# Three transfers of a recurrence's substitution step, issued on GpSimd's queue and no longer on SyncE's

## Chip, cores and metric

The kernel runs on one core of a Trainium2 chip. The metric is the device time of one execution in microseconds (us), given as the median of several runs; lower is better.

## What is computed

The reference runs two blocks of two layers each on 512 tokens of width 1024 in float32. The part that matters here is the first layer of the second block: a recurrence over the tokens with 12 heads of size 64, run forwards and backwards, over 256 context tokens and then 512 more.

```python
def rwkv7_scan(r, w, k, v, kk, bb, s0, reverse):
    def step(s, inp):
        r_t, w_t, k_t, v_t, kk_t, b_t = inp
        sa = jnp.einsum('bhij,bhj->bhi', s, kk_t)
        s = s * w_t[:, :, None, :] - sa[..., None] * b_t[:, :, None, :] + v_t[..., None] * k_t[:, :, None, :]
        return s, jnp.einsum('bhij,bhj->bhi', s, r_t)
```

The rest (projections, gated normalisations, a windowed attention, a pooling layer, two feed-forward layers and a retention layer) lies before and after this stage.

## The kernel before

The program is written with a layer that takes the engine of every instruction from the code, adds the waits between instructions itself and chooses, at build time, the order in which each engine meets its instructions. Every engine works through its own queue in that order. All transfers of the kernel are issued by SyncE (`nc.sync`).

The recurrence (`rwkv`, L1288) works in chunks of 64 tokens. Two heads form a pair; there are six pairs, and each pair has three groups of four chunks for each of the two directions, which makes 18 passes, numbered from 0 here. The loop at L1401 runs pass q: it weaves, one step of each in turn, the chain of states of pass q (`chain`, L1797), the second half of the inversion for pass q+1 (`inner_rest`, L1691, and `inner_second`, L1740), the products of pass q+2 (`products`, L1634, and `keys_by_token`, L1678) and the vectors of pass q+3 (`inner_first`, L1567). The recurrence inside a chunk asks for the inverse of 16 triangular systems of size 64 x 64 (two directions, two heads, four chunks). Between these, `Feed` (L2120) puts matmuls of the projections of later pairs (L363 to L365), whose weight panels are loaded at L349 into two buffers `ws`.

One inversion takes this way. TensorE makes the products (L1648), VectorE masks them into `M` (L1652). SyncE stores the 16 systems to a scratch tensor `lt` in device memory (L1659, two transfers) and loads from it the 64 diagonal blocks of 16 x 16, one on each of 64 partitions, into `sN` (L1662). GpSimd inverts these by substitution: thirty operations (L1670, L1671) on `sX`, `sO` and `sN`, which have one buffer each, after two operations that set `sX` to the unit matrix (L1665, L1666). It then writes the transposed copy `sT` (L1664, called at L1673). Both are stored to a scratch tensor `td` (L1675, `sT` first in the code). One step of the weaving later, `inner_rest` loads `td` back as 64 x 64 matrices, `T` from the transposed one and `DB` from the other, two transfers each (L1733). GpSimd also clears `VU` in that function (L1701, two operations), which has two buffers and so waits for products of an earlier `chain` (L1862). `inner_second` completes the inverse from the blocks with matmuls of L1757: the first group multiplies with `T`, the second with `DB`. `chain` uses the result.

Of the kernel before, what the change touches and what calls it, by code (L numbers as in the profile page):

```python
# [273 lines left out]
class Program:  # L274
# [1013 lines left out]
    def rwkv(self, hl, hc):  # L1288
# [3 lines left out]
        with tc.tile_pool(name="rk", bufs=1) as rp:  # L1292
# [176 lines left out]
            def leading():  # L1469

                for j, tags in enumerate((("acc0", "acc1"), ("acc0", "c"), ("u", "c"))):
                    lead.append([self.psum(t)[:, :n] for t, n in zip(tags, (T, TC))])
                    for p0, ks in ((0, (0, 1, 2, 3)), (4, (4, 6, 7))):
                        pan = self.panel(out[j], p0, 4)
                        for k in ks:
                            products(j, pan, p0, (k,))
                            yield
# [6 lines left out]
            for j in range(3):  # L1484
                products(j, self.panel(out[j], NH2 - 1, 1), NH2 - 1, (NH2 - 1,))
# [148 lines left out]
    def products(self, g, st):  # L1634

        nc, rp = self.nc, self.rp
        tt = nc.vector.tensor_tensor
        half = lambda i: slice(64 * i, 64 * i + 64)

        M = st["M"] = rp.tile([P, 2, 2, 4, P], F32, tag="m", name="m", bufs=3)  # L1640

        e2 = lambda ap: ap.rearrange("p (c e) t -> p c e t", e=2)
        for d in range(2):
            pss, last = [self.psum("c", (P, 4, P)) for _ in range(2)], None
            for j in range(4):
                i = 2 - 2 * (j % 2)
                for h in (1, 0):
                    last = self.queue(nc.tensor.matmul(  # L1648
                        pss[h][:, j, :], st["BK"][d][half(h), j, :, :].rearrange("p s t -> p (s t)"),
                        st["AR"][d][half(h), j // 2, i:i + 2, :].rearrange("p s t -> p (s t)"), start=True, stop=True), last)  # L1650
            for h in range(2):
                tt(out=e2(M[:, d, h]), in0=e2(pss[h]), in1=self.k_pmask[:, d].unsqueeze(1).to_broadcast([P, 2, 2, P]), op=ALU.mult)  # L1652
                yield

        lt, td = self.scratch[self.flip]
        self.flip = 1 - self.flip
        system = lambda e: M.rearrange("p d h (j e) t -> p e (d h) j t", e=2)[half(1 - e), e, :, :, half(e)]
        for e in range(2):
            nc.sync.dma_start(out=lt[e::2, :4096].rearrange("u (s t) -> s u t", t=64), in_=system(e))  # L1659
        N, X, XT, o = (rp.tile([64, 16, 16], F32, tag=t, name=t) for t in ("sN", "sX", "sT", "sO"))  # L1660
        blocks = lambda ap: ap.rearrange("u (b f) -> (u b) f", f=1040)[:, :1024].rearrange("q (s t) -> q s t", t=64)[:, :, :16]
        nc.sync.dma_start(out=N, in_=blocks(lt))  # L1662
        pt = nc.gpsimd.tensor_tensor
        copy = lambda out, in_: nc.gpsimd.tensor_scalar(out=out, in0=in_, scalar1=1.0, scalar2=None, op0=ALU.mult)  # L1664
        nc.gpsimd.memset(X, 0.0)  # L1665
        nc.gpsimd.memset(X.rearrange("p s t -> p (s t)")[:, ::17], 1.0)  # L1666
        for j in range(15, 0, -1):
            ob = o[:, :j, :16 - j]
            sh = [64, j, 16 - j]
            pt(out=ob, in0=N[:, :j, j:j + 1].to_broadcast(sh), in1=X[:, j:j + 1, j:].to_broadcast(sh), op=ALU.mult)  # L1670
            pt(out=X[:, :j, j:], in0=X[:, :j, j:], in1=ob, op=ALU.subtract)  # L1671

        copy(XT, X.rearrange("p s t -> p t s"))  # L1673
        for k, x in ((1, XT), (0, X)):
            nc.sync.dma_start(out=blocks(td[k]), in_=x)  # L1675
        st["td"], st["system"] = td, system

    def keys_by_token(self, st):  # L1678
# [543 lines left out]
```

## Time and profile before

| | |
|---|---|
| median of 3 runs | 2342.03 us (2341.47 to 2350.18) |
| profiled execution | 2327.58 us |
| its span, first to last instruction | 2325.8 us |
| mean granted TensorE clock | 0.971 |
| TensorE busy | 2169.9 us (93%) |
| VectorE busy | 1623.5 us (70%) |
| ScalarE busy | 1077.7 us (46%) |
| GpSimd busy | 343.7 us (15%) |
| transfers | 269.66 MB, all but 2.57 MB of instructions on SyncE's queue |

PE is TensorE's matmuls, PEld its weight loads, DVE VectorE, ACT ScalarE, POOL GpSimd and SP SyncE; a q behind an engine's name is its queue (SPq). Issuing a transfer is not counted as busy. `T<-td` reads: `T` is written, `td` is read. L12 is line 12 of the kernel. All times of the trace are counted from the start of the span.

### The profile page before, as it was taken

To read this page: it belongs to the slowest core of one execution; us is meant where nothing else is said; L and a number is where in the kernel's file an instruction comes from. 1 tells how busy PE (TensorE), PEld (TensorE's weight loads), DVE (VectorE), ACT (ScalarE), POOL (GpSimd) and SP (SyncE) were. 2 spreads that over 40 slices of the span, in tenths; PEclk is the share of its full clock that TensorE was granted. 3 is DMA by queue.
4 is the path that set the end of the run, shared out by engine and by line. 5 is a ranking of instruction groups with operands and counts; after the bars stand their busy time and mean duration, and the time that the engine had idled before them with its cause. 6 is when DMAs were issued, how large, how long until landed. Compare 5 with 4: busy or idle time off the path is not lost. (4 is left out here: it accounts for less than half of the span.)

```text
span 2325.8 us, 40219 instructions
## 1 busy us (share of the span) xinstructions
PE 2169.9 (93%) x15774; PEld 1735.8 (75%) x15774; DVE 1623.5 (70%) x3014; ACT 1077.7 (46%) x2033; POOL 343.7 (15%) x722
## 2 busy tenths in 40 slices
PE   6889989999998999999988998999999999999996
PEld 4667768878775888888666776777777777888885
DVE  6799886568859688444666868778867456555544
ACT  3466353223344332333554556546465255655542
POOL 1321020000003000000003443332424100000001
PEclk9999999999999999999999999989999999999998
DMA  8433446566623656323333232322222252422211
GB/s 288 145 128 127 135 152 197 180 220 194 193 76 115 217 187 201 109 92 90 115 100 76 44 74 47 70 46 62 56 50 54 85 177 90 131 68 73 73 55 46
DMA packets 203742, 269.66 MB, mean 116 GB/s; under 512 B 125216, under 2 KB 137376, under 8 KB 203168
## 3 DMA queue, kind: packets, MB, share of 16 engines
q1 hardware_dynamic: 203552, 267.09, 37.9%
q8 instruction: 124, 2.03, 0.4%
q14 instruction: 66, 0.54, 0.1%
HBM read 250.38 MB, written 16.66 MB: 115 GB/s over the span
## 5 line engine op out<-in xcount | busy, mean ns | idle before, releaser
L363 PE MATMUL acc<-hh,wh 128*128 128x512 f32 x1416 | 572.2, 405 | 39.6 <-ACT wh L322 24.9
L365 PE MATMUL acc<-hh,wl 128*128 128x512 f32 x1416 | 569.9, 403 | 8.0 <-POOL wl L340 4.6
L364 PE MATMUL acc<-hl,wh 128*128 128x512 f32 x1416 | 570.9, 403 | 1.8 <-DVE hl L340 1.7
L322 ACT ACTIVATE wh<-ws 128x1024 fp32r<-128x1024 f32 (+4 forms) x307 | 275.5, 901 | 412.0 <-PE acc L364 309.7
L340 DVE TENSOR_TENSOR wl<-ws,wh 128x1024 fp32r<-128x1024 f32 (+3 forms) x294 | 305.3, 1041 | 189.4 <-ACT wh L322 185.8
L363 PEld LDWEIGHTS acc<-hh,wh 128*128 128x128 f32 x1416 | 270.2, 191 | 100.1 <-ACT wh L322 28.1
L365 PEld LDWEIGHTS acc<-hh,wl 128*128 128x128 f32 x1416 | 270.0, 191 | 74.0 <-DVE wl L340 8.0
L364 PEld LDWEIGHTS acc<-hl,wh 128*128 128x128 f32 x1416 | 270.8, 191 | 60.0 <-issue 6.3
L447 DVE SCALAR_TENSOR_TENSOR ws<-ws,cact 128x1024 f32<-128x1024 f32 x144 | 180.5, 1256 | 78.1 <-DMA ws<-in_ada_dram 77.2
L363 PE MATMUL acc<-gh,wh 128*128 128x512 f32 x352 | 137.9, 392 | 2.4 <-ACT gh L322 2.4
L365 PE MATMUL acc<-gh,wl 128*128 128x512 f32 x352 | 138.1, 392 | 1.8 <-DVE wl L340 1.8
L364 PE MATMUL acc<-gl,wh 128*128 128x512 f32 x352 | 138.0, 392 | 0.3 <-DVE gl L340 0.3
L322 ACT ACTIVATE a<-a 128x512 f32<-128x512 f32 x44 | 27.8, 633 | 186.4 <-DVE a L988 186.1
L1670 POOL TENSOR_TENSOR sO<-sN,sX 64x15 f32<-64x15 f32 (+2 forms) x270 | 84.8, 314 | 182.3 <-DMA sN<-lt 162.9
L1671 POOL TENSOR_TENSOR sX<-sX,sO 64x15 f32<-64x15 f32 (+2 forms) x270 | 87.1, 322 | 21.0
L2025 POOL TENSOR_TENSOR raw<-raw,k_axial 128x512 f32<-128x512 f32 x16 | 21.9, 1366 | 413.9 <-ACT raw L322 413.9
L365 PEld LDWEIGHTS acc<-gh,wl 128*128 128x128 f32 x352 | 66.5, 189 | 16.8 <-DVE wl L340 3.1
L363 PEld LDWEIGHTS acc<-gh,wh 128*128 128x128 f32 x352 | 66.5, 189 | 16.6 <-ACT gh L322 2.8
L364 PEld LDWEIGHTS acc<-gl,wh 128*128 128x128 f32 x352 | 66.5, 189 | 14.7 <-DVE gl L340 1.0
L447 DVE SCALAR_TENSOR_TENSOR ada<-ws,cact 128x1024 f32<-128x1024 f32 x48 | 58.7, 1222 | 25.9 <-DMA ws<-in_ada_dram 25.8
L1848 DVE SCALAR_TENSOR_TENSOR S<-sp,gc,gs 64x64 f32<-64x64 f32 x240 | 58.7, 279 | 21.1 <-PE sp L1840 19.1
L363 PE MATMUL acc<-hc,wh 128*128 128x256 f32 x208 | 66.3, 319 | 4.2 <-ACT wh L322 3.8
(581 smaller groups left out, 4308.8 us busy)
## 6 DMA issues: line engine op xcount, KB each, us to landing
ws<-in_ada_dram SPq DMA_DIRECT2D x144, 512.0 KB, 4.3
ws<-in_up_dram SPq DMA_DIRECT2D x88, 512.0 KB, 4.1
ws<-in_od_in_dram SPq DMA_DIRECT2D x44, 512.0 KB, 3.5
ws<-in_ev_in_dram SPq DMA_DIRECT2D x60, 256.0 KB, 2.9
ws<-in_down_dram SPq DMA_DIRECT2D x32, 384.0 KB, 3.1
ws<-in_w_in_dram SPq DMA_DIRECT2D x22, 512.0 KB, 4.3
ws<-in_down_dram SPq DMA_DIRECT2D x32, 320.0 KB, 3.0
ws<-in_ev_in_dram SPq DMA_DIRECT2D x18, 512.0 KB, 3.5
```

What stands on the lines that cost most here:

```text
L322: ins = self.nc.scalar.activation(out=out, in_=in_, func=func, **k)
L340: (engine or self.nc.vector).tensor_tensor(out=lo, in0=x, in1=hi.bitcast(F32), op=ALU.subtract)
L363: nc.tensor.matmul(ps, wh[:, s], xh, start=start, stop=False)
L364: nc.tensor.matmul(ps, wh[:, s], xl, start=False, stop=False)
L365: nc.tensor.matmul(ps, wl[:, s], xh, start=False, stop=stop)
L447: nc.vector.scalar_tensor_tensor(out=w, in0=ws, scalar=1.0, in1=c, op0=ALU.mult, op1=ALU.mult, accum_out=d[:, m:m + 1])
L1670: pt(out=ob, in0=N[:, :j, j:j + 1].to_broadcast(sh), in1=X[:, j:j + 1, j:].to_broadcast(sh), op=ALU.mult)
L1671: pt(out=X[:, :j, j:], in0=X[:, :j, j:], in1=ob, op=ALU.subtract)
L1848: nc.vector.scalar_tensor_tensor(out=nxt[H, d, H], in0=sp[H, d], scalar=gd, in1=gs[H, d, H], op0=ALU.mult, op1=ALU.add)
L2025: nc.gpsimd.tensor_tensor(out=raw, in0=raw, in1=self.k_axial[:, 0, :], op=ALU.mult)
```

## The change

The load of the diagonal blocks (`sN` from `lt`) and the two stores of the inverted blocks (`sT` and `sX` to `td`) are issued by GpSimd. The order in the code, the buffers, the shapes and all other transfers stay as they are; the stores to `lt` (L1659) and the loads `T` and `DB` from `td` (L1733) stay on SyncE.

```diff
         N, X, XT, o = (rp.tile([64, 16, 16], F32, tag=t, name=t) for t in ("sN", "sX", "sT", "sO"))
         blocks = lambda ap: ap.rearrange("u (b f) -> (u b) f", f=1040)[:, :1024].rearrange("q (s t) -> q s t", t=64)[:, :, :16]
-        nc.sync.dma_start(out=N, in_=blocks(lt))
+        nc.gpsimd.dma_start(out=N, in_=blocks(lt))
...
         copy(XT, X.rearrange("p s t -> p t s"))
         for k, x in ((1, XT), (0, X)):
-            nc.sync.dma_start(out=blocks(td[k]), in_=x)
+            nc.gpsimd.dma_start(out=blocks(td[k]), in_=x)
```

## Rows read from the trace of the kernel before

**Rows 1.** Busy time by engine (x instructions), granted clock, DMA share, GB/s; recurrence stage

```profile
1210.00:1840.00 630.00, 587.09 (x8102) 453.54 (x8103) 480.79 (x1178) 334.61 (x773) 214.80 (x624) 0.94 0.27 61
```

**Rows 2.** Waits of engines in 1210:1840: us in total, times, longest us

```profile
PE c L1757 <- DMA T<-td: 12.9, 10, 5.3
...
ACT wh L322 <- DMA ws<-in_ev_in_dram: 2.1, 1, 2.1
```

**Rows 3.** Timeline of TensorE, L1757: start, us, in brackets the idle time before

```profile
1246.57 0.42 PE L1757 MATMUL c<-T,LB 64*64 64x32 f32 x2 [5.35 <-DMA T<-td]
...
1548.40 1.91 PE L1757 MATMUL c<-T,LB 64*64 64x32 f32 x30 [1.05 <-DMA T<-td]
1553.50 0.75 PE L1757 MATMUL c<-EC,DB 64*64 64x32 f32 x10
...
1817.75 0.27 PE L1757 MATMUL c<-T,LB 64*64 64x32 f32 x2 [1.88 <-DMA T<-td]
```

**Rows 4.** Chain of work that ended last, pass 9: start us, us, what

```profile
1521.23 0.61 DVE m L1652
...
1522.51 2.61 DMA lt<-m
...
1525.18 2.61 DMA sN<-lt
...
1540.18 1.34 POOL sT L1664
1541.54 2.50 DMA td<-sT
...
1544.69 3.67 DMA T<-td
1548.40 1.91 PE c L1757 x30
```

**Rows 5.** SyncE's waits in 1210:1840: us in total, times, longest us

```profile
SPq L1675 <- POOL sX L1671: 130.0, 16, 17.2
...
SPq L1662 <- DMA lt<-m: 23.1, 13, 2.8
...
SPq L1675 <- POOL sT L1664: 15.8, 17, 7.0
```

**Rows 6.** Issues by line: ns min/median/max; then landing of L1659, of L1662 (us)

```profile
L1659 SPq DMA_DIRECT2D lt<-m x36: 589/626/671, 1219.3 to 1792.2; - x36
...
DMA to landing us min/median/max: 2.6/2.7/3.7
...
L1662 SPq DMA_DIRECT2D sN<-lt x18: 586/592/1111, 1223.3 to 1795.1; - x18
...
DMA to landing us min/median/max: 2.6/2.9/4.3
```

**Rows 7.** Timeline of SyncE: issues of passes 3 and 4

```profile
1311.84 0.59 SPq L1662 DMA_DIRECT2D sN<-lt  x1
...
1339.08 1.28 SPq L1659 DMA_DIRECT2D lt<-m  x2
...
1344.41 0.60 SPq L1662 DMA_DIRECT2D sN<-lt  x1
```

**Rows 8.** Single operations of GpSimd and VectorE from timeline and line view (copy: ns)

```profile
1318.25 0.22 POOL L1670 TENSOR_TENSOR sO<-sN,sX 64x15 f32<-64x15 f32 x1
...
1257.30 0.30 POOL L1670 TENSOR_TENSOR sO<-sN,sX 64x64 f32<-64x64 f32 x1
1257.67 0.31 POOL L1671 TENSOR_TENSOR sX<-sX,sO 64x64 f32<-64x64 f32 x1
...
L1664 POOL TENSOR_SCALAR sT<-sX x18: 1060/1074/1335, 1240.0 to 1811.1; 64x256 f32<-64x256 f32 x18
...
1353.30 1.01 DVE L1631 SCALAR_TENSOR_TENSOR ks<-r,pcol,ks 128x768 f32<-128x768 f32 x1
1353.41 1.06 POOL L1671 TENSOR_TENSOR sX<-sX,sO 64x64 f32<-64x64 f32 x1
```

**Rows 9.** Timeline of GpSimd, first operations of passes 0, 1, 3 and 17

```profile
1226.50 0.40 POOL L1670 TENSOR_TENSOR sO<-sN,sX 64x15 f32<-64x15 f32 x1 [62.93 <-DMA sN<-lt]
...
1252.43 0.22 POOL L1670 TENSOR_TENSOR sO<-sN,sX 64x15 f32<-64x15 f32 x1 [9.38 <-DMA sN<-lt]
...
1317.18 1.09 POOL L1701 MEMSET VU<- 64x512 f32 x2 [19.16 <-PE misc L1862]
...
1798.11 0.44 POOL L1670 TENSOR_TENSOR sO<-sN,sX 64x15 f32<-64x15 f32 x1 [9.23 <-DMA sN<-lt]
```

## The prediction

> **What bounds the kernel now.** I first read the busy times by stage. The only stage that runs the changed lines is the recurrence, from 1210 to 1840 us. There TensorE is busy 587.09 of 630 us and GpSimd 214.80 [rows 1], so this stage holds 43 us of TensorE idle time, and the change can neither win more than that nor touch the rest of the program. Next I read the waits of the stage: TensorE waits 12.9 us for the transfer `T<-td`, ten times, and only 2.1 us can be laid to a weight panel that came late (ScalarE's wait on `ws`) [rows 2]. The ten waits belong to eight of the eighteen passes; the timeline has the first at 1246.57 and the last at 1817.75 [rows 3]. The other ten passes show no wait for it.
>
> Then the chain of work that ended last, which goes back no further than 1521 us. It opens with a pass of the substitution: mask product, store to `lt`, load of `sN`, thirty GpSimd operations, the copy to `sT`, store to `td`, load of `T`, and the first matmuls of L1757: 27.2 us from 1521.23 to 1548.40 with nothing beside it [rows 4]. All three moved transfers belong to this path, two of them directly: `sN<-lt` and `td<-sT`.
>
> Last, SyncE's own waits. It stands 130.0 us waiting for the last subtraction, 15.8 us for the copy to `sT` and 23.1 us for `lt` to land [rows 5]. That looks like much, but SyncE is not what the stage waits for: the late panels above come to 2.1 us.
>
> **The change, part by part.** Each pass moves three issues, 54 in all.
>
> 1. *Off SyncE.* 54 issues of 0.59 us [rows 6] are 32 us of SyncE's time, and the waits of rows 5 go with them. Part of these waits moves to the next in line: the loads `T<-td` and `DB<-td` stay on SyncE and need the stores landed. Queued behind a waiting SyncE are panel loads, the loads of saved context and `lt` stores. What these cost TensorE now is the 2.1 us above, and once `sN` is asked for late in one of the eight passes: the second store to `lt` goes out at about 1339.7, lands some 2.7 us later [rows 6], and the load follows only at 1344.41 [rows 7], 2.0 us late. The gain is 4 us.
>
> 2. *Onto GpSimd.* Each transfer has 1,024 pieces of 64 bytes (64 partitions of 16 rows of 16 numbers). No row shows GpSimd issuing one. Let g be the time one issue takes there, and x = g - 0.59 what it adds to the path. At the cheap end g is SyncE's own 0.59 us, x = 0. By GpSimd's plain operations, 0.22 us for 15 elements and 0.30 for 64 [rows 8], a step is 1.6 ns, and 1,024 steps with a start of 0.2 us make g = 1.9. By its transposing copy, 1.07 us for 256 elements [rows 8], a step is 3.4 ns after the same start, g = 3.7 and x = 3.1. If the reading and the writing side are made one after the other, g = 7.2 and x = 6.6: the dear end. Making a list of scattered addresses lies between the plain operation and the copy, so I take 2.8 us, x = 2.2 (estimates from these rows).
>
>  The queue choice has a price in the Trainium skill too (DMA: Bandwidth & Descriptors, "Latency and other measured facts"): first byte after about 1 us when GpSimd issues, against about 0.6 from SyncE's kind of queue; no run so far shows it here. By that page x would be 0.4 and the sum below about 1 us.
>
> 3. *The load of `sN`.* GpSimd now waits for `lt` itself. What stands behind that wait, the two clearings of `VU` and the thirty operations, stood behind the wait on `sN` before. In five of the eight passes GpSimd is idle until `sN` lands (the first and the last stand in [rows 9]), so x counts fully: 5x. In the other three GpSimd is held by the clearing of `VU`, which waits for TensorE: in the first of them `sN` is asked for at 1311.84, lands 2.9 us later, and the clearing ends at 1318.27 [rows 6, 7, 9], which covers x up to 3.5. I take these three at nothing; without that cover they cost 3x.
>
> 4. *The store of `sT`* comes right behind the copy on GpSimd and delays `T` by x in all eight passes: 8x.
>
> 5. *The store of `sX`* now goes second, so `DB` lands about g after `T`. The first product that reads `DB` begins at 1553.50, 5.1 us after the products with `T` start [rows 3]: covered up to g of about 5. The clearing of `sX` for the next pass waits longer for this store; in pass 1 GpSimd idles 9.38 us after that clearing [rows 9], against 2 × 2.8 us of new issues. Covered, and gone where g passes 4 or so.
>
> Sum: 13x - 4 = 13 × 2.2 - 4 = 25 us. The profiled execution took 2327.58 us, 1.8 more than its span of 2325.8, and would take 2352; it lies 14.5 below the median of the runs, 2342.03, so against that I forecast **2367 us**, 1.1% slower. At x = 0 the sum is -4 (2338), at 3.1 it is +36 (2378). At the dear end the covers of parts 3 and 5 go as well: 16 × 6.6 - 4 = 102 (2444).
>
> **Rivals.** Half a per cent, 11.7 us, is what a measurement here can tell from no change; all chances below use it.
>
> *No change* (2338 to 2353). GpSimd issues about as cheaply as SyncE, x below 1.2; 13 × 1.2 - 4 = 12. Or the build, which orders TensorE's queue by its own estimate of arrivals, puts other matmuls ahead of L1757; then the path is longer but TensorE is not idle. Against it: the 27 us of rows 4 are serial, and TensorE has only this stage's projections left to put there. The page named above supports this rival. 0.27. Should the change not do what it says (GpSimd's transfers served just as SyncE's are), it ends here too.
>
> *Faster.* SyncE free of 169 us of waits lets `lt` stores and loads go earlier, and TensorE's waits for `T` vanish with the late panel: 12.9 + 2.1 = 15, to 2327. It decides where an issue on GpSimd is cheaper than the hop to SyncE, that is with x below about -0.6. For it: the size of rows 5. Against it: in the traced pass the store starts 0.02 us after the copy ends, and the load starts 0.65 us after the store has landed, of which 0.59 is its own issue [rows 4, 6], so there is hardly a hop to save. 0.13.
>
> *Much slower* (2444). The issue on GpSimd is held up or made in two rounds. GpSimd's operations are already stretched beside VectorE: the 64-element subtraction that takes 0.31 us alone took 1.06 while VectorE ran L1631 for 1.01 [rows 8]. If each issue waited like that, 0.75 us more, x rises to 3.0 and the sum to 35. The Trainium skill (SBUF — State Buffer, "SBUF: two separate sides") says that GpSimd cannot write its transfer descriptors while VectorE holds the port that they share; the stretched row agrees for operations, and none shows it for transfers. Only with the dear end of part 2 does it become 102. 0.15.
>
> *My forecast*, slower by 12 to 75 us: 0.45.
>
> **The numbers.** Slower holds forecast and dear rival, 0.60; same 0.27; faster 0.13. The range goes from 2328, which leaves out about half of the faster rival, to 2430, which leaves out most of the dear one: about 2 in 10 outside. Its own part for the likeliest case is 2354 to 2417.
>
> **What would show it.** In the changed profile GpSimd's queue should show 54 issues, their mean being g; 0.6 kills part 2, above 4 makes the dear rival. From the end of the copy to the landing of `td<-sT`, now 2.5 us, should be 2.5 + x. TensorE's waits for `T` should grow from 12.9 by about 13x = 29, or, if the order of the build took it up, stay while the stage still grows. SyncE's waits of rows 5 should turn into waits of L1733 for `td`. I am wrong if the stage keeps its 630 us with g above 2, or if it shrinks: then SyncE's standing still did cost TensorE something that the waits lay elsewhere.

## The result, and the profile after

The changed kernel took 2376.45 us (median of 4 runs, 2372.21 to 2381.43) against 2341.75 us for the kernel before on the same chip (median of 4): the ratio is 1.0139, with a 95% interval of 1.0099 to 1.0179. It is 34.7 us slower. Ratios and intervals, here and below, come from the runs in the chip's usual state alone and are not the quotients of the medians, from which they differ by up to 0.2%. The profiled executions differ by more, 2372.21 against 2327.58 us, because the one of before lies 14 us below its median and the other only 4.

All of it is in the recurrence. From 1210 us to the first use of `T` in the last pass the kernel before takes 608 us. This is the row of before for that stretch (columns as in [rows 1]: length, busy time of TensorE, its weight loads, VectorE, ScalarE, GpSimd, then the granted clock, DMA share and GB/s), with two later slices in which the clock is at its lower level:

```profile
1210.00:1818.00 608.00, 565.09 (x7794) 436.32 (x7794) 471.35 (x1153) 329.59 (x759) 214.80 (x624) 0.95 0.26 59
...
1540.00:1550.00 10.00, 7.93 (x95) 6.04 (x91) 6.90 (x20) 4.45 (x12) 1.85 (x4) 0.92 0.55 107
1550.00:1560.00 10.00, 10.00 (x137) 8.49 (x135) 5.18 (x13) 3.77 (x11) 3.21 (x11) 0.50 0.12 22
1560.00:1570.00 10.00, 10.00 (x67) 8.09 (x69) 4.45 (x11) 2.08 (x3) 7.14 (x23) 0.50 0.00 0
```

And this is the changed kernel, up to the same point, with the slices around its pass 9:

```profile
1210.00:1863.00 653.00, 589.03 (x7816) 455.34 (x7816) 472.70 (x1160) 331.45 (x763) 261.60 (x678) 0.91 0.24 55
...
1560.00:1570.00 10.00, 5.94 (x61) 4.14 (x59) 6.12 (x19) 4.35 (x11) 3.95 (x8) 0.97 0.40 72
1570.00:1580.00 10.00, 9.81 (x128) 8.43 (x128) 4.14 (x10) 3.13 (x9) 1.81 (x3) 0.50 0.17 43
1580.00:1590.00 10.00, 10.00 (x170) 8.62 (x170) 6.06 (x15) 3.65 (x7) 6.55 (x20) 0.85 0.05 11
```

The stage is 45 us longer. TensorE's idle time (length less busy time) goes from 42.9 to 64.0, 21 us more. Its busy time goes from 565.1 to 589.0, 24 us more, for the same matmuls: 565.09 x 0.95 and 589.03 x 0.91 are both about 537 us of work at full clock (2.4 GHz). So the loss has two parts, standing still and running slowly, and in the slices shown the second follows the first: the slice with 5.94 us busy is followed by one at 0.50, which is 1.2 GHz. The kernel before ran slowly behind this pass too, for two slices; what tells the kernels apart is the mean of the stage, 0.95 against 0.91. In the medians the second part is smaller than in the profiles: of 34.7 us some 14 would be left for it, if the idle time is the 21 us of the profiles (an estimate).

The idle part is the wait for `T`. The waits of TensorE, GpSimd and SyncE in the changed kernel, from 1210 to 1900 us (us in total, times, longest; to be held against [rows 2, 5]):

```profile
PE c L1757 <- DMA T<-td: 32.9, 14, 7.4
...
POOL VU L1701 <- PE misc L1862: 179.8, 12, 34.3
POOL sN L1662 <- DMA lt<-m: 144.7, 9, 60.2
POOL sO L1670 <- DMA sN<-lt: 39.8, 17, 3.7
...
SPq L1733 <- DMA td<-sX: 132.2, 13, 18.2
...
SPq L1733 <- DMA td<-sT: 31.7, 16, 10.4
```

TensorE's wait for `T` rose from 12.9 to 32.9 us. It stands before the first use of `T` in passes 0, 3, 6, 9, 12, 15, 16 and 17, of which these are 9 and 12 from TensorE's timeline (the brackets hold the idle time before), each with the 30 matmuls behind it, and pass 6 for comparison; the last line is pass 12 in the kernel before:

```profile
1459.81 0.27 PE L1757 MATMUL c<-T,LB 64*64 64x32 f32 x2 [1.17 <-DMA T<-td]
1460.44 1.11 PE L1757 MATMUL c<-T,LB 64*64 64x32 f32 x30 [0.36 <-DMA T<-td]
...
1569.10 0.27 PE L1757 MATMUL c<-T,LB 64*64 64x32 f32 x2 [3.27 <-DMA T<-td]
1570.19 1.91 PE L1757 MATMUL c<-T,LB 64*64 64x32 f32 x30 [0.82 <-DMA T<-td]
...
1679.84 0.39 PE L1757 MATMUL c<-T,LB 64*64 64x32 f32 x2 [4.67 <-DMA T<-td]
1680.94 1.91 PE L1757 MATMUL c<-T,LB 64*64 64x32 f32 x30 [0.72 <-DMA T<-td]
```

```profile
1658.72 1.11 PE L1757 MATMUL c<-T,LB 64*64 64x32 f32 x30 [0.53 <-DMA T<-td]
```

After 1.17 us of idle time the thirty matmuls take 1.11 us, after 3.27 and 4.67 us they take 1.91. The length of one wait does not settle it: in the kernel before they took 1.91 us after 1.05 us in pass 9 [rows 3]. The waits grew most in three passes: from 0.53 to 5.39 us in pass 12, from 1.50 to 5.48 in pass 15 and from nothing to 3.22 in pass 16, together 12.1 of the 20.0 us.

Why is `T` late? The issues of the two lines, for the load and then for the stores (as in [rows 6]: ns minimum, median and maximum; then landing in us):

```profile
L1662 POOL DMA_DIRECT2D sN<-lt x18: 820/820/1017, 1223.6 to 1836.1; - x18
...
DMA to landing us min/median/max: 2.8/2.9/4.4
...
L1675 POOL DMA_DIRECT2D td<-sX x18: 878/889/894, 1241.5 to 1855.7; - x18
L1675 POOL DMA_DIRECT2D td<-sT x18: 831/834/843, 1242.4 to 1856.6; - x18
...
DMA to landing us min/median/max: 2.9/3.0/4.8
```

One issue on GpSimd takes 0.82 to 0.89 us, not much more than SyncE's 0.59 [rows 6]. The chain that ended last shows what else there is; this is its part in pass 9, to be read beside [rows 4] (start us, us, what):

```profile
1542.11 2.60 DMA lt<-m
1545.25 2.83 DMA sN<-lt
...
1562.06 0.89 POOL td L1675
1562.94 2.97 DMA td<-sT
1566.57 3.58 DMA T<-td
1570.19 1.91 PE c L1757 x30
```

From the landing of `lt` to the issue of `sN` it is 0.54 us (1544.71 to 1545.25), before 0.06; the load takes 2.83 us, before 2.61. The copy to `sT` is done at 1562.06, but the store of `sX` is issued first, 0.89 us, and then the store of `sT` takes 2.97 us, before 2.50. That is 0.7 us for the load and 1.36 us for the store: 2.1 us on the path of this pass.

In some passes there is more. GpSimd's timeline in pass 12:

```profile
1656.07 0.52 POOL L1701 MEMSET VU<- 64x512 f32 x1 [28.43 <-PE misc L1862]
1656.57 0.82 POOL L1662 DMA_DIRECT2D sN<-lt  x1
1657.43 0.52 POOL L1701 MEMSET VU<- 64x512 f32 x1
1659.58 0.22 POOL L1670 TENSOR_TENSOR sO<-sN,sX 64x15 f32<-64x15 f32 x1 [1.63 <-DMA sN<-lt]
```

The load stands behind the clearing of `VU` in GpSimd's queue, and the clearing waits for TensorE. In the kernel before SyncE asked for `sN` during that wait, and in the same pass the substitution began right behind the clearing:

```profile
1637.74 1.09 POOL L1701 MEMSET VU<- 64x512 f32 x2 [29.21 <-PE misc L1862]
1638.81 0.22 POOL L1670 TENSOR_TENSOR sO<-sN,sX 64x15 f32<-64x15 f32 x1
```

Now issue and landing come after it: 3 us from the end of the first clearing to the substitution. Eight of the eighteen loads stand like this, in passes 4, 6, 7, 10, 12, 13, 15 and 16; nine wait for `lt` (144.7 us, 9 times), one for neither. Passes 12, 15 and 16 are those in which the wait for `T` grew most. In pass 3, which was covered before as well, the build set the load ahead of the clearing:

```profile
1319.15 0.82 POOL L1662 DMA_DIRECT2D sN<-lt  x1 [14.96 <-DMA lt<-m]
1324.00 1.09 POOL L1701 MEMSET VU<- 64x512 f32 x2 [4.03 <-PE misc L1862]
```

There the cover held, and the wait for `T` grew by 1.3 us only, about what the stores add.

### The profile page after: what moved, and what is told of

Same layout as the page of the kernel before. It is cut to its first block, busy times and chain, and to the rows that moved or that the text cites. A ratio compares the mean times of both kernels' runs of the same rounds, so it can differ in the third digit from the quotient of the medians.

```text
span 2370.4 us, 40248 instructions
## 1 busy us (share of the span) xinstructions
PE 2194.9 (93%) x15774; PEld 1755.3 (74%) x15774; DVE 1622.8 (68%) x3014; ACT 1078.3 (45%) x2033; POOL 388.1 (16%) x776
## 5 line engine op out<-in xcount | busy, mean ns | idle before, releaser
L1757 PE MATMUL c<-T,LB 64*32 64x32 f32 (+1 forms) x1152 | 43.5, 228 | 33.0 <-DMA T<-td 32.9
```

What stands on the lines that cost most here:

```text
L1757: nc.tensor.matmul(ps[64 * i + r0:64 * i + r0 + m, x, :], lhs(x, half(i)), rhs(x, half(i)), start=True, stop=True)
```

## Experiments

Every kernel below was timed against the kernel before on its own chip: medians 2337.05 us for the first four, 2335.85 for the next four, 2339.53 and 2341.16 for the two pairs of the last part. Microseconds lost or won are worked out from the ratio below (1.0139 for the changed kernel is 33 us).

| kernel | median us | ratio | 95% interval |
|---|---|---|---|
| load of `sN` alone on GpSimd | 2369.35 | 1.0120 | 1.0069 to 1.0171 |
| the two stores alone on GpSimd | 2349.65 | 1.0056 | 1.0018 to 1.0094 |
| changed, `VU` cleared by VectorE | 2366.41 | 1.0103 | 1.0070 to 1.0137 |
| before, `VU` cleared by VectorE | 2345.41 | 1.0027 | 0.9996 to 1.0057 |
| changed, store of `sT` first | 2380.39 | 1.0169 | 1.0119 to 1.0218 |
| before, copy to `sT` made three times | 2363.27 | 1.0127 | 1.0078 to 1.0176 |
| store of `sX` alone on GpSimd | 2353.53 | 1.0067 | 1.0032 to 1.0101 |
| load alone, `VU` cleared by VectorE | 2361.82 | 1.0120 | 1.0076 to 1.0164 |
| changed, 24 matmuls in the waits | 2407.00 | 1.0283 | 1.0245 to 1.0321 |
| before, 24 matmuls in the waits | 2412.24 | 1.0301 | 1.0259 to 1.0342 |
| changed, 8 matmuls in the waits | 2347.63 | 1.0026 | 0.9999 to 1.0054 |
| before, 4 matmuls in the waits | 2322.99 | 0.9911 | 0.9879 to 0.9943 |

### Which transfer

Load alone:

```diff
-        nc.sync.dma_start(out=N, in_=blocks(lt))
+        nc.gpsimd.dma_start(out=N, in_=blocks(lt))
```

> The kernel before with one line changed: only the load of sN is issued by GpSimd; the stores of sT and sX stay on SyncE. Queue theory (the load now stands in GpSimd's queue behind the clearing of VU, which waits for TensorE's products of L1862, so that in the passes where the clearing is last the 3 us of issue and landing come after it and no longer beside it): most of the loss of 34 us is here, 15 to 25 us slower than before, with GpSimd's waits for sN after the clearing near 3 us in five or six passes. Path theory (each moved transfer merely takes longer, this one by about 0.7 us): 8 passes x 0.7, 4 to 8 us slower. SyncE theory (the loss comes from SyncE standing at the loads of T and DB in front of the next stores to lt): no slower than before, since the stores to td are still issued there.

Stores alone:

```diff
-            nc.sync.dma_start(out=blocks(td[k]), in_=x)
+            nc.gpsimd.dma_start(out=blocks(td[k]), in_=x)
```

> The kernel before with one line changed: only the two stores to td are issued by GpSimd, the load of sN stays on SyncE. Queue theory: a minor part of the loss, since nothing of GpSimd's stands in front of these stores; only the extra path of about 1.4 us a pass (the issue of sX ahead of sT, 0.89 us, and a landing slower by 0.5 us), so 6 to 12 us slower. Path theory: two thirds of the loss, 20 us or more. SyncE theory: nearly the whole loss of 34 us, with stores to lt that go out 4 to 6 us after M is ready, as in passes 13, 16 and 17 of the changed kernel.

Measured: 28 us and 13 us slower than before, both a little above the ranges of the queue theory (15 to 25 and 6 to 12). Both parts cost, the load about twice what the stores do. SyncE's new place of waiting, at the loads from a `td` that another engine stores, is not the cause: the larger loss comes where SyncE still issues these stores. So far the queue theory looked best.

### What stands ahead of the load in GpSimd's queue

Changed kernel, and kernel before, each with this edit:

```diff
-            nc.gpsimd.memset(VU[half(1 - e), :, e::2, :], 0.0)
+            nc.vector.memset(VU[half(1 - e), :, e::2, :], 0.0)
```

> The changed kernel with one line changed: VectorE clears VU, GpSimd no longer does, so that the load of sN has no waiting operation ahead of it in GpSimd's queue. Queue theory: gives back 15 to 25 us of the 34, to some 12 to 20 us slower than before; GpSimd issues the load within 1 us of the landing of lt in all passes. Path theory: nothing comes back, 30 to 36 us slower than before. SyncE theory: nothing comes back either. Beside these, VectorE takes over 36 clearings and may itself stand in front of TensorE's wait; the control with the kernel before has the same edit and says what that is worth.

> The control of the run above: the kernel before with VectorE clearing VU. Queue theory: in the kernel before the load of sN goes on SyncE beside the clearing, so taking the clearing off GpSimd is worth only what it stood behind the load by, 1 to 2 us in each of five passes (1.2 in pass 12, 2.1 in pass 16): 0 to 8 us faster. Path theory and SyncE theory: no difference, within 4 us. If the waiting of VectorE for TensorE does harm, it shows here as a slower run, and is to be taken off the run above.

And the load alone with the same edit:

> The kernel before with the load of sN issued by GpSimd and the clearing of VU given to VectorE: the load alone, without the waiting operation ahead of it in GpSimd's queue. To be held against the load alone (28 us slower than before) and against the clearing on VectorE alone (6 us slower). Queue theory: the load then costs only its 0.75 us of path, 6 to 8 us, so 12 to 15 us slower than before. If the load costs the same with and without the clearing ahead of it: 28 to 34 us slower.

Measured: 24, 6 and 28 us slower than before. The edit did in the trace what it should. GpSimd's wait ahead of the load and TensorE's for `T` in the changed kernel with this edit, 1210 to 1900 us:

```profile
POOL sN L1662 <- DMA lt<-m: 330.8, 17, 61.3
```

```profile
PE c L1757 <- DMA T<-td: 20.5, 10, 6.7
```

Now 17 of 18 loads wait for `lt` and none for the clearing. Of the 20.0 us by which the waits for `T` had grown, 12.4 are gone; passes 12, 15 and 16 hold 4.1 us in place of 14.1. In the trace, then, more than half of the added wait comes from the load's place behind the clearing.

The times are less clear. Of the 33 us 9 came back. But the control is slower by 6 us itself, and its expectation says that this is to be taken off: 18 us of the change are left with the clearing out of the way, so 15 came back, as the queue theory had it. The load alone costs the same ratio with and without the clearing ahead of it, 1.0120; held against the control 22 us are left (0.93%, where 6 to 8 us were expected), so 6 of 28 came back. With the intervals of the table put together, the first figure lies between 1 and 29 us and the second between -11 and 24. So the queue order is real in the trace, and its price in time is not shown: it may be small, or most of the loss.

### Which store goes first

Changed kernel, with the order of issue fixed (an order between two instructions of one queue, without a wait):

```diff
-            nc.gpsimd.dma_start(out=blocks(td[k]), in_=x)
+            st["o"] = self.queue(nc.gpsimd.dma_start(out=blocks(td[k]), in_=x), None if k else st["o"])
```

> The changed kernel with the order of the two stores fixed, sT first. Path theory (each microsecond on the path from M to T costs about 9 us of the whole: the stores alone made the path 1.35 us longer a pass and cost 13 us): taking the 0.85 us by which the issue of sX stands ahead of sT off the path gives back 8 us, to about 25 us slower than before. Queue theory in its pure form (all of the loss from the load standing behind the clearing of VU): nothing comes back, 33 us slower. If sX going second delays DB so that it is waited for: no gain either, with waits of TensorE for DB in its place.

Measured: 1.0169 against 1.0139 for the changed kernel, with intervals that overlap. The 8 us did not show. The order took less off the path than the 0.85 us reckoned: by GpSimd's timeline the store of `sT` goes out 1.37 us after the start of the copy in place of 1.92 (medians of 18), 0.55 us earlier. The wait for `T` was 26.2 us in its trace and not 32.9, but the timed runs were no faster. Inconclusive.

Kernel before, with the store of `sX` alone moved:

```diff
-            nc.sync.dma_start(out=blocks(td[k]), in_=x)
+            (nc.sync if k else nc.gpsimd).dma_start(out=blocks(td[k]), in_=x)
```

> The kernel before with only the store of sX issued by GpSimd, behind the copy to sT; the load of sN and the store of sT stay on SyncE. Path theory: nothing of the path to T changes, DB lands about 1.5 us later than now and has several microseconds to spare: within 4 us of before. SyncE theory, turned round (SyncE's 130 us of waiting for the last subtraction do harm): these waits go, so it is faster by 4 us or more. If DB has no room to spare: slower by 8 us or more, with waits for DB.

Measured: 16 us slower. The first two expectations missed, and the third had the time but not the reason: TensorE never waits for `DB`. The chain of this kernel has this step:

```profile
1565.05 3.49 DMA td<-sT
```

The store of `sT`, still on SyncE, now takes 3.5 us and not 2.50 [rows 4]. Both stores now go out at the same moment, when the copy is done; before, the one of `sX` went out a microsecond earlier, during the copy. The Trainium skill (DMA: Bandwidth & Descriptors, "Issuing engines are not separate DMA queues") says that transfers issued by different engines run on the same DMA engines and that only time of the issuing queue is saved; this run agrees, with 1 us lost. The expectation that the path stays as it is was false: it grew by 1 us in this pass, and TensorE's waits for `T` went from 12.9 to 20.1 us. Nor was SyncE freed; it stood 147.8 us for the copy to `sT` in place of 130.0 us for the last subtraction [rows 5].

### A pure delay

Kernel before, all transfers on SyncE:

```diff
-        copy(XT, X.rearrange("p s t -> p t s"))
+        for _ in range(3): copy(XT, X.rearrange("p s t -> p t s"))
```

> The kernel before, all transfers on SyncE, with the transposing copy to sT made three times, which puts 2 x 1.07 = 2.1 us of pure delay on the path of every pass and changes no queue. This is as much as the moved transfers add by themselves (0.75 for the load, 1.35 for the stores). Path theory: 8 to 9 us for each microsecond, so 17 to 21 us slower than before, half of it as waits for T and half as matmuls stretched by a lower granted clock. If the delay is all there is to the change: 30 us or more. If only the queues matter: under 5 us.

Measured: 30 us slower, 1.27%. Its stage up to the first use of `T` in the last pass, and the waits there:

```profile
1210.00:1851.00 641.00, 581.95 (x7811) 449.77 (x7811) 476.55 (x1161) 332.49 (x765) 257.44 (x660) 0.92 0.25 56
```

```profile
PE c L1757 <- DMA T<-td: 27.2, 14, 6.4
```

That is more than the 17 to 21 us expected of the path. The delay itself came out longer than 2.1 us: from the start of the first copy to the store of `sT` it is 3.53 us in place of 1.10 (medians of 18 passes), so 2.4 us. A delay that changes no queue costs about what the whole change costs, and in the same two parts: 16 us more of idle time (59.0 against 42.9) and 17 us more of busy time at a clock of 0.92. One microsecond on the path of every pass costs about 12 us of the whole. By this rate the 2.1 us which the transfers bring with them are worth some 25 of the 33 us. With the lost cover of three passes added the eight passes have 23 us of delay (worked out below, where the prediction is gone through) in place of the 19 of this run (8 x 2.4), which makes 35. The interval of the change, 23 to 42 us, holds both: a late `T` is enough to explain the loss, and how much of it the queue order brings is not decided here either.

### The clock

If a wait costs a second time through the clock, then a TensorE that does useless work during the wait should win. The edit adds a method and calls it ahead of the first products with `T`; `XT` and the pass number are kept in `st`:

```diff
+        self.fill(st, (0, 3, 6, 9, 12, 15, 16, 17) , 24)
         E, EC = self.E[0], rp.tile([P, 8, 32], F32, tag="gs", name="EC")
...
+    def fill(self, st, passes, n):
+        if st["q"] in passes:
+            ps, x, last = self.psum("c", (P, 256)), st["XT"].rearrange("p s t -> p (s t)"), None
+            for _ in range(n):
+                last = self.queue(self.nc.tensor.matmul(ps, x[:, :P], x, start=True, stop=True), last)
```

> The changed kernel with 24 matmuls added in front of the first products with T, in the eight passes whose wait for T is 1 us or more (0, 3, 6, 9, 12, 15, 16, 17). They multiply the copy sT with itself into an accumulator that nobody reads, so TensorE has work in the stretch in which it would stand still; T arrives when it did. Clock theory (the wait itself is half of the loss: the profiled run of the changed kernel has 21 us more of idle TensorE in the stage, and 24 us more of busy time for the same matmuls at a granted clock of 0.91 and no longer 0.95): the clock of the stage comes back to 0.94 or more and 10 to 24 us are won, to some 10 to 25 us slower than before. If the clock does not follow the waits: nothing is won, and the 24 matmuls (2.6 us at full clock) cost up to 10 us where they push useful ones back.

The kernel before with the same method and the call `self.fill(st, (0, 3, 4, 6, 9, 12, 15, 17) , 24)`:

> The kernel before with the same 24 matmuls, in the passes in which its trace shows a wait for T (0, 3, 4, 6, 9, 12, 15, 17). Its own waits for T are shorter, 12.9 us in all, so more of the added 8 x 2.6 = 21 us lies beside useful work. Clock theory: the stage has 565 us of busy TensorE at a granted clock of 0.95; at 1.00 this would be 537, so up to 28 us are there to win, against some 8 to 10 us that the matmuls cost beyond the waits: 0 to 18 us faster than before. If the clock does not follow the waits: 5 to 21 us slower.

Measured: 66 and 70 us slower, a miss by size. The 24 matmuls are 48 in the trace and took 10.62 us in pass 9, not 2.6:

```profile
1570.99 10.62 PE L2123 MATMUL c<-sT 64*128 64x256 f32 x48
```

Still the pair says something. With so much work in front, `T` lands 5 to 34 us before its use in every pass of both kernels, no wait for it is left, and then the changed kernel is not slower than the kernel before (2407.00 against 2412.24 us; the intervals leave room for some 9 us). So the change costs little or nothing where `T` is not waited for.

Then the right size, 8 for the changed kernel and 4 for the kernel before:

```diff
-        self.fill(st, (0, 3, 6, 9, 12, 15, 16, 17) , 24)
+        self.fill(st, (0, 3, 6, 9, 12, 15, 16, 17) , 8)
```

> The changed kernel with 8 of these matmuls and not 24, in the same eight passes. In the run with 24 one of them took 0.43 us at full clock, four times what was reckoned, so that 24 filled 10 us where a wait is 1.2 to 7.4 us; 8 take 3.5 us, 28 us in all against 30 us of waits. Clock theory: the waits are filled at hardly any cost and the clock of the stage rises from 0.91 to 0.94 or more: 10 to 20 us are won, to 14 to 24 us slower than before. If the stretches at the low clock come whether TensorE waits or not: no gain, 33 to 43 us slower than before, and the clock stays at 0.91 to 0.92.

```diff
-        self.fill(st, (0, 3, 4, 6, 9, 12, 15, 17) , 24)
+        self.fill(st, (0, 3, 4, 6, 9, 12, 15, 17) , 4)
```

> The kernel before with 4 of these matmuls in each of the eight passes in which it waits for T, 1.7 us at full clock, 14 us in all against its 12.9 us of waits. Clock theory: the clock of the stage rises above 0.95 and up to 15 us are won; with some matmuls beside useful work 0 to 15 us faster than before. If the clock does not follow: 3 to 14 us slower.

Measured: the changed kernel with 8 is 6 us slower than before, so 27 of the 33 us came back, more than the 10 to 20 expected. The stage of this kernel and its waits:

```profile
1210.00:1840.00 630.00, 592.64 (x7941) 456.69 (x7941) 476.78 (x1175) 338.25 (x777) 259.99 (x678) 0.96 0.24 57
```

```profile
PE c L2123 <- POOL sT L1664: 4.3, 1, 4.3
...
PE c L1757 <- DMA T<-td: 0.7, 2, 0.4
```

The clock is 0.96 and not 0.91, and the mean over the program is 0.970 to 0.975 in all twelve timed runs, against 0.951 to 0.958 for the changed kernel on its chip. The added matmuls are 33.7 us of the 592.6; the others take 559, 30 us less than in the changed kernel. Their work is the same, and an issue on GpSimd takes as long as before (0.82 to 0.90 us, one 1.02). One thing beside the matmuls differs: in this build only three loads, of passes 6, 12 and 15, stand behind a clearing, and no longer eight, so a part of the 27 us may belong to that.

The kernel before with 4 of them is 21 us **faster** than the kernel before, ratio 0.9911, more than the 15 us expected at most, and the fastest of all kernels here. Its stage, and slices around its pass 9:

```profile
1210.00:1816.00 606.00, 573.46 (x7892) 440.94 (x7891) 477.98 (x1175) 337.60 (x777) 213.86 (x624) 0.97 0.26 60
...
1550.00:1560.00 10.00, 10.00 (x186) 8.07 (x185) 8.54 (x24) 4.31 (x11) 1.52 (x5) 1.00 0.44 98
1560.00:1570.00 10.00, 10.00 (x151) 8.30 (x151) 9.42 (x19) 5.99 (x13) 8.28 (x23) 1.00 0.01 2
1570.00:1580.00 10.00, 10.00 (x98) 7.94 (x97) 9.26 (x22) 3.52 (x7) 2.82 (x9) 1.00 0.58 111
```

And TensorE's timeline there:

```profile
1551.70 1.99 PE L2123 MATMUL c<-sT 64*128 64x256 f32 x8
1553.62 1.12 PE L1757 MATMUL c<-T,LB 64*64 64x32 f32 x32
```

Before, pass 9 was followed by 20 us at 0.50, and 30 matmuls of this group took 1.91 us [rows 3]; here 2 us of useless work precede 32 matmuls in 1.12 us, and the clock stays at 1.00. The two profiled runs differ by only 2 us in the stage, since the one of before is among its better ones (its clock is 0.971); the gain rests on the timed runs, whose mean clock is 0.969 to 0.980 against 0.956 to 0.972 for the kernel before on the same chip. The control with the matmuls in passes that do not wait was not tried, so part of the gain could be this build's order; that the clock rises with the waits filled is shown.

## Why the prediction came out right in time and partly wrong in cause

The forecast was 25 us slower, 2367 us; measured were 34.7 us and 2376.45. The sign, the stage, the path and the range hold. Its steps do not all hold.

1. *Off SyncE, a gain of 4 us: not found.* SyncE's waits went to the next in line, as the step said: 163.9 us at L1733 for `td` (132.2 + 31.7), where the kernel before had 24.7 there and 168.9 at the lines that were moved [rows 5], so only some 30 us of waiting went away. No run shows a gain from it; but no run isolates it either.

2. *Onto GpSimd, g = 2.8 us and x = 2.2: the term that was mis-sized.* Measured are 0.82 to 0.89 us, so x is 0.23 to 0.30. The estimate read a DMA issue as if GpSimd handled its pieces one by one at the pace of its vector operations; that pace does not apply. By the forecast's own formula 13 x 0.3 - 4 gives 0, and the condition of the rival "no change" (x below 1.2) was met. Yet the time did not stay. The sentence on the Trainium skill's page (DMA: Bandwidth & Descriptors, "Latency and other measured facts") with its 0.4 us was nearer for the single transfer: the store of `sT` takes 0.47 us longer, the load 0.22.

3. *The load, 5x, with three passes covered: the cover failed in two of them and in a new one.* The step said that what stands behind GpSimd's wait stood there before, and took the three passes with a clearing of `VU` (3, 12 and 15) at nothing. It overlooked that the build may set the load itself behind that clearing, so that its 3 us come after it. This happened in passes 12 and 15, and in pass 16, which now waits as well; in pass 3 the load went first and the cover held. In passes without a clearing ahead the load costs 0.7 us, more than x, because of the 0.5 us from landing to issue.

4. *The store of `sT`, 8x: right in place, larger than x.* 0.47 us by itself.

5. *The store of `sX` goes second: wrong.* The build sends it first, which puts 0.89 us in front of `sT`. That is more than the slower store itself. The code's order was taken for the order of issue, although before, too, SyncE sent `sX` first in 17 of 18 passes (the first two stores at 1240.0 and 1241.2 us), where it was hidden beside the copy.

With measured terms the forecast's sum is 4 x 0.7 for the load, 3 x 3 for the lost cover and 8 x 1.36 for the stores, 23 us. TensorE's waits for `T` rose by 20.0 (29 were forecast), the idle time by 21. So this way of counting passes and waits was sound, and that an over-dear issue came to the same sum as the hops, the order and the lost cover was luck.

6. *What the sum had no term for: the clock.* It priced a microsecond of waiting at one microsecond. The longer busy time comes on top, 24 us in the profiles and some 14 in the medians, and the run with 8 matmuls, which fills the waits, gives 27 us back. The rows for it were there: TensorE's 30 matmuls in pass 9 took 1.91 us [rows 3], and the stage stood at 0.94 [rows 1]. The Trainium skill (TensorE: Matmul & The Clock Gate, "HAM oscillation — how this bites in real kernels") describes a matmul loop in which each wait for a transfer lets the clock fall anew; this trace agrees, with seven of the eight waits followed by such a group of 30 matmuls in 1.80 to 1.91 us, and one in 1.11; in the kernel before it is three of eight (1.73 to 1.92).

One reading of the prediction is to be put right: the 0.65 us from the landing of the store to the load of `T`, "of which 0.59 is its own issue", are the issue of the first of the two loads of `T`, which stands ahead of the second; that there is hardly a hop holds.

Of the rivals, "much slower" is out: the 36 stores were issued in 831 to 894 ns, without one that was held up, although VectorE was busy 472 us of the 653. What the Trainium skill (SBUF — State Buffer, "SBUF: two separate sides") says of transfers beside VectorE no run here shows. "Faster" asked for an issue cheaper than SyncE's, and there is none.

Open is why the load alone costs 28 us. By the pure delay's 12 us for each microsecond its 0.7 us should cost 8. With the clearing on VectorE the load alone is 22 us slower than its control, with an interval of 9 to 34, so the 8 lie just outside. These are the stage and the waits for `T` of that kernel, and then of its control:

```profile
1210.00:1855.00 645.00, 590.20 (x7793) 451.76 (x7791) 490.31 (x1197) 333.92 (x769) 215.51 (x610) 0.91 0.24 56
```

```profile
PE c L1757 <- DMA T<-td: 14.1, 8, 5.2
```

```profile
1210.00:1839.00 629.00, 578.01 (x7782) 442.95 (x7778) 487.08 (x1189) 330.68 (x761) 197.91 (x592) 0.93 0.25 57
```

```profile
PE c L1757 <- DMA T<-td: 13.8, 8, 5.8
```

The waits for `T` are nearly equal, and 12 of the 16 us are busy time at a lower clock (both profiled executions are the slowest of their kernel). So here the clock is lower without a longer wait for `T`, and what lowered it no run shows; the account by waits for `T` holds for the whole change and not for this part of it. Also open is what the queue order costs in time, and whether sending `sT` first is worth anything: the traces show both, the timed runs do not.

## What to carry to other kernels

On a path that ends in a wait of TensorE, count every hop and every issue ahead in the same queue, not only the transfer that moved; and price the wait that results at one and a half to two times its length where the row behind it shows the lower clock. Before moving a transfer to another queue, look at what that queue waits for just then: a load behind a waiting instruction loses the time that it used to hide. Where a wait of a few microseconds cannot be removed, matmuls of about its length whose result nobody reads can win more than they cost, and lose when they are longer than the wait.

## What the runs showed of the hardware that was not expected

- The issue of a transfer of 1,024 pieces of 64 bytes holds GpSimd for 0.82 to 0.89 us, in 54 issues with one load at 1.02 as the longest; SyncE's takes 0.58 to 0.59 us at the median.
- Two such stores that go out at the same time on two queues land after 3.5 us at the median; a microsecond apart on SyncE's queue alone 2.5 us.
- The time of one and the same kernel goes with TensorE's mean granted clock: 2328.00 us at 0.971 and 2358.31 us at 0.955 for the kernel before on one chip. A clock lower by 0.016 makes 35 us of its 2170 us of busy TensorE; the two are 30 us apart.
- A matmul of 64x128 by 64x256 in float32 shows as two in the trace and takes 0.44 us (24 of them 10.62 us), four times what had been reckoned.
